# A hybrid attention and state space step: the pair mixing's Pool half on DVE, the norms' low parts on DVE, sums of squares by two additions

## The chip, the cores and the metric

One core of a Trainium2 chip runs the whole step. Its engines are TensorE (PE in the rows, PEld for its weight loads), VectorE (DVE), ScalarE (ACT), GpSimd (Pool) and SyncE (SP, which here issues the transfers). The metric is the device time of one execution in microseconds (us). Results are compared as medians of several runs.

## What is computed

One layer of a streaming encoder on 16 learned meta tokens, 2048 prompt frames and 64 new frames, 1024 wide, float32:

```python
q, k, v, u = project(h, p)            # pre-RMSNorm and one input projection
attn = swa_prompt(q, k, v, sinks)     # windowed attention, 8 query heads, 2 kv heads
y_ssm, fr, fi = s5_scan(u, h0_re, h0_im, p)   # 32 channel groups, each a 64-wide complex diagonal state
zs = gelu(y_ssm)
s_out = zs * sigmoid(zs @ w_glu + b_glu)
merged = concatenate([rmsnorm(attn, attn_out_g), rmsnorm(s_out, ssm_out_g)])
h = h + merged @ w_out
h = h + square(relu(rmsnorm(h, norm2_g) @ w_up)) @ w_down
```

The state space part is x[t] = a x[t-1] + B u[t] with complex a, then y = Re(C x) + D u. The kernel scans blocks of 8 tokens: 266 blocks (`NCH`), 258 of the prompt (`PCH`) and 8 of the new frames, which start from a given state.

## The kernel before

Products keep float32 accuracy by splitting each operand into a high part, rounded on ACT, and a low part, the difference between value and high part, and multiplying high by high, high by low and low by high. A low part is thus one two-input subtraction in SBUF on DVE or Pool.

The program runs through stages: the projection of u; attention, with the q, k, v projection, the tables of the state space part and the first products with `w_out`; the state space pairs; the gate (GLU) with the rest of the products with `w_out`; then the squared-ReLU MLP, more than half of the time.

The stage of the pairs works on sixteen pairs of channel groups. For pair j, SP loads U and `ra` (`ssm_load`: two matrices and two tables, a cosine and a sine for each block) and `rb` (`ssm_load2`). PE multiplies U into block inputs (`ssm_in`, L1244), ACT copies them from PSUM into `RI` (`ssm_align`, L1253). Then `ssm_mix(j, i)` runs in six steps. Step 0 multiplies `RI` by the cosine table (`o1`, L1263, DVE) and the sine table (`o2`, L1264, Pool), 2 x 266 columns each. Step 1 combines them into real and imaginary part (`ab`, L1266 on DVE, L1267 on Pool). Steps 2 and 3 scan each part along the blocks, 258 columns and then 8 (L1271, DVE). Step 4 multiplies the result by the two tables again (`p1`, L1275, DVE; `p2`, L1276, Pool). Step 5 writes H, the states at the block ends: two subtractions into partitions 0 to 63 (L1281, DVE), two additions into partitions 64 to 127 (L1284, Pool), and then two small copies on DVE (L1286, L1287). PE multiplies H and U into the output (`ssm_out`, L1293 and L1294), ACT copies it (L1299), SP stores it. `ssm_mixes` writes the steps of pair i among those of pair i - 1:

```python
for j, k in ((i, 0), (i - 1, 4), (i, 1), (i, 2), (i - 1, 5), (i, 3)):
```

Between the pairs PE fills its time with products of the attention half with `w_out`: `out` (L1452) sums an output tile in PSUM, `out_evac` adds it on DVE into `xo` (L1494), SP stores two of them together (L1455) and loads the next buffer (L1445). There are three `xo` buffers.

The norms ahead of `w_out` run on six blocks of 352 tokens, for the attention half ("a") and the gated half ("s"). `norm_square` squares on ACT (L1406) and sums four slices on DVE (L1408), PE sums over partitions (L1413), `norm_root` and `norm_newton` form the inverse root, and `norm_split` multiplies (L1434, DVE), rounds (L1435, ACT) and takes the low part (L1436, Pool), each twice per block, 704 columns. `wg_split` splits the gate's weights: high part on ACT (L1392), low part on Pool (L1393), two of 1024 columns.

The order of the instructions on each engine is not the order of writing: `Order.arrange` collects them all, gives each a cost by engine, size and kind, lets operations of DVE and Pool that share SBUF inputs exclude each other in time, and places them by a list schedule run backwards and forwards. A changed engine therefore means a new order for the whole program. SP, too, issues its transfers in that order, one behind the other.

Of the kernel before, what the change touches and what calls it, by code (L numbers as in the profile page):

```python
# [15 lines left out]
ALU = mybir.AluOpType  # L16
AX = mybir.AxisListType
# [31 lines left out]
def f32(ap):  # L49
    return ap.bitcast(F32)  # L50
# [326 lines left out]
def tile_trunk(ctx: ExitStack, tc: tile.TileContext, I, O, dbg=None, stop=None):  # L377
    nc = tc.nc
# [375 lines left out]
    xr, xh, xl, ss, rs = {}, {}, {}, {}, {}  # L754
# [500 lines left out]
    def ssm_mix(j, i):  # L1255

        x, sp, v, e = Sx[j], Sx["sp"], nc.vector, nc.gpsimd
        two = lambda a: a.unsqueeze(1).broadcast_to((P, 2, NCH))
        tc_, ts_ = two(x["ra"][:, 2 * P : 2 * P + NCH]), two(x["ra"][:, 2 * P + NCH :])
        wide = lambda n: sp.tile([P, 2, NCH], F32, tag=n, name=n)  # L1260
        if i == 0:
            x["o1"], x["o2"], x["ab"] = (wide(n) for n in ("o1", "o2", "ab"))
            v.tensor_mul(x["o1"], x["RI"], tc_)  # L1263
            e.tensor_mul(x["o2"], x["RI"], ts_)  # L1264
        elif i == 1:
            v.tensor_add(x["ab"][:, 0], x["o1"][:, 0], x["o2"][:, 1])  # L1266
            e.tensor_sub(x["ab"][:, 1], x["o1"][:, 1], x["o2"][:, 0])  # L1267
        elif i in (2, 3):
            c = i - 2
            for lo, hi, init in ((0, PCH, 0.0), (PCH, NCH, g0[:, c, j : j + 1])):  # L1270
                v.tensor_tensor_scan(out=x["ab"][:, c, lo:hi], data0=r8[:, j : j + 1].broadcast_to((P, hi - lo)),  # L1271
                                     data1=x["ab"][:, c, lo:hi], initial=init, op0=ALU.mult, op1=ALU.add)
        elif i == 4:
            x["p1"], x["p2"] = wide("p1"), wide("p2")
            v.tensor_mul(x["p1"], x["ab"], tc_)  # L1275
            e.tensor_mul(x["p2"], x["ab"], ts_)  # L1276
        elif i == 5:
            H = x["H"] = GH[j % 2]
            for gg in range(2):
                r = slice(64 * gg, 64 * gg + 64)  # L1280
                v.tensor_sub(H[0:64, gg, 1:], x["p1"][r, 0], x["p2"][r, 1])  # L1281
            for gg in range(2):
                r = slice(64 * gg, 64 * gg + 64)
                e.tensor_add(H[64:, gg, 1:], x["p1"][r, 1], x["p2"][r, 0])  # L1284
            gs = slice(2 * j, 2 * j + 2)
            v.tensor_copy(Sx["fin"][:, :, gs].rearrange("p q g -> p g q"), H[:, :, PCH : NCH + 1 : NCH - PCH])  # L1286
            v.tensor_copy(H[:, :, PCH], Sx["h0"][:, gs])  # L1287
# [27 lines left out]
    def ssm_mixes(i):  # L1315

        for j, k in ((i, 0), (i - 1, 4), (i, 1), (i, 2), (i - 1, 5), (i, 3)):
            if pair_ok(j):
                ssm_mix(j, k)
# [69 lines left out]
    def wg_split(k):  # L1389
        h, l = (w[:, 2 * k : 2 * k + 2] for w in WO["g"])  # L1390
        raw = WO.pop(("g", k))
        nc.scalar.copy(h, raw)  # L1392
        nc.gpsimd.tensor_sub(l, raw, f32(h))  # L1393

    def norm_x(t, n):
        x = WO["na"].tile([P, 4, OB], F32, tag="x", name="x")
# [6 lines left out]
    def norm_square(t, n):  # L1403
        x = N[t, n]
        sq = WO["na"].tile([P, 4, OB], F32, tag="x", name="sq")
        nc.scalar.activation(sq, x["x"], AF.Square)  # L1406
        x["ss"] = WO["na"].tile([P, OB], F32, tag="t", name="ss", bufs=1)
        nc.vector.tensor_reduce(out=x["ss"], in_=sq.rearrange("p k n -> p n k"), axis=AX.X, op=ALU.add)  # L1408

    def norm_sum(t, n):  # L1410
        x = N[t, n]
# [16 lines left out]
    def norm_split(t, n):  # L1428
        x = N[t, n]
        a, y = x.pop("x"), x.pop("y")  # L1430
        h, l = (WO["na"].tile([P, 4, OB], F32R, tag="x" + i, name="x" + i) for i in "hl")
        x["h"], x["l"] = h, l
        for ks in (slice(0, 2), slice(2, 4)):
            nc.vector.tensor_mul(a[:, ks], a[:, ks], y.unsqueeze(1).broadcast_to((P, 2, OB)))  # L1434
            nc.scalar.copy(h[:, ks], a[:, ks])  # L1435
            nc.gpsimd.tensor_sub(l[:, ks], a[:, ks], f32(h[:, ks]))  # L1436

    hv = hd.rearrange("e p n -> p e n")
    
# [86 lines left out]
    for t, f in ((26, a2_open), (27, lambda: norm_square("a", 0)), (28, lambda: norm_sum("a", 0)), (28, lambda: norm_root("a", 0)), (28, lambda: norm_newton("a", 0)),  # L1526
                 (28, wo_open), (29, lambda: norm_split("a", 0)), (28, lambda: wo_split(0, 0)), (28, lambda: wo_split(0, 1)),
                 (29, lambda: wo_split(0, 2)), (29, lambda: wo_split(0, 3)), (29, lambda: norm_load(1)), (30, lambda: wg_row(0)), (30, lambda: wg_row(1)), (31, lambda: norm_square("a", 1)),
                 (31, lambda: wg_split(0)), (32, lambda: wg_split(1)), (32, lambda: norm_sum("a", 1)), (32, lambda: norm_root("a", 1)), (33, lambda: norm_newton("a", 1)), (33, lambda: norm_split("a", 1))):
        jobs.setdefault(t, []).append(f)  # L1530
# [8 lines left out]
    for s in range(NC_ + 2):  # L1539
# [47 lines left out]
        for f in jobs.get(s, ()):  # L1587
# [15 lines left out]
    Sx["pr"] = lambda: prs.tile([P, OB], F32, tag="r", name="psr")  # L1603
    norm_load(2)
    do = {"load": norm_load, "square": lambda n: norm_square("a", n), "sum": lambda n: norm_sum("a", n),
          "root": lambda n: norm_root("a", n), "newton": lambda n: norm_newton("a", n), "split": lambda n: norm_split("a", n)}
    after = {}
    for i, fs in ((-2, "square 2"), (-1, "sum 2, root 2"), (0, "newton 2, split 2, load 3"), (2, "square 3"), (3, "sum 3, root 3"),
# [227 lines left out]
    v, e = nc.vector, nc.gpsimd  # L1836
# [421 lines left out]
```

## Time and profile before

| what | us |
|---|---|
| median of 3 runs | 2190.11 (2185.74 to 2190.66) |
| profiled execution | 2188.35, its span 2186.6 |
| PE busy | 2030.3 (93%) |
| DVE busy | 1888.7 (86%) |
| ACT busy | 1259.2 (58%) |
| Pool busy | 592.9 (27%) |
| stage of the pairs, 485 to 656 | 171, of it DVE busy 151.6, PE 133.8, Pool 107.6 |

Busy time is the time in which at least one instruction of the engine runs; an engine can be busy and yet wait inside an instruction. A row of groups gives line, engine, operation, output and inputs, shape and count, then busy time and mean length of one (ns), then the idle time of the engine ahead of the group and what ended it. A row of a source line gives shortest, median and longest execution in ns. A row of a timeline gives start and length in us.

### The profile page before, as it was taken

To read this page: it belongs to the slowest core of one execution; us is meant where nothing else is said; L and a number is where in the kernel's file an instruction comes from. 1 tells how busy PE (TensorE), PEld (TensorE's weight loads), DVE (VectorE), ACT (ScalarE), POOL (GpSimd) and SP (SyncE) were. 2 spreads that over 40 slices of the span, in tenths; PEclk is the share of its full clock that TensorE was granted. 3 is DMA by queue.
4 is the path that set the end of the run, shared out by engine and by line. 5 is a ranking of instruction groups with operands and counts; after the bars stand their busy time and mean duration, and the time that the engine had idled before them with its cause. 6 is when DMAs were issued, how large, how long until landed. Compare 5 with 4: busy or idle time off the path is not lost.

```text
span 2186.6 us, 35316 instructions
## 1 busy us (share of the span) xinstructions
PE 2030.3 (93%) x12230; PEld 1950.7 (89%) x12230; DVE 1888.7 (86%) x3378; ACT 1259.2 (58%) x2560; POOL 592.9 (27%) x670
## 2 busy tenths in 40 slices
PE   8989989898866997999999999999999999999999
PEld 7978888787655996999989989999999999999999
DVE  8969999988985787899999998888977988888778
ACT  6447777863325463665555566665555765555554
POOL 7943211035660434554334441200000200000000
PEclk9999999989988997999999999999999999999999
DMA  6532223447662466654564667645744774444432
GB/s 220 136 67 80 69 74 86 151 156 225 225 196 69 126 194 216 201 190 151 175 219 164 225 210 248 202 144 161 254 152 140 223 226 138 136 140 137 142 122 92
DMA packets 306164, 354.46 MB, mean 162 GB/s; under 512 B 28737, under 2 KB 216768, under 8 KB 305474
## 3 DMA queue, kind: packets, MB, share of 16 engines
q1 hardware_dynamic: 305842, 352.21, 51.4%
q8 instruction: 97, 1.59, 0.3%
q14 instruction: 81, 0.66, 0.1%
q10 hardware_dynamic: 144, 0.00, 0.0%
HBM read 260.15 MB, written 94.07 MB: 162 GB/s over the span
## 4 chain that ended last, share of the span: by engine, by line
PE 58%; DVE 26%; DMA 5%; issue 5%; ACT 4%; SPq 1%; POOL 0%; DVEq 0%; ACTq 0%; POOLq 0%
PE psd L2066 24%; PE bB L1971 9%; PE bA L1971 8%; PE bC L1971 7%; PE pso L1452 3%; DVE acc L2075 2%; DVE ul L1961 2%; PE psqkv L906 2%; DVE hl L2054 2%; PE psg L1670 1%; PE pu L811 1%; DMA hd<-xo 1%; DVE M L1142 1%; PE pv L1184 1%; DVE wl L2035 1%
## 5 line engine op out<-in xcount | busy, mean ns | idle before, releaser
L2066 PE MATMUL psd<-hh,wh 128*128 128x352 f32 x1344 | 434.6, 324 | 11.6 <-DVE acc L2075 10.0
L2066 PE MATMUL psd<-hl,wh 128*128 128x352 f32 x1344 | 431.7, 322 | 2.1 <-DVE hl L2054 1.9
L2066 PE MATMUL psd<-hh,wl 128*128 128x352 f32 x1344 | 429.9, 321 | 0.2 <-DVE wl L2035 0.2
L2075 DVE TENSOR_TENSOR acc<-psd,acc 128x352 f32<-128x352 f32 x624 | 315.2, 517 | 36.5 <-PE psd L2066 36.1
L2066 PEld LDWEIGHTS psd<-hh,wh 128*128 128x128 f32 x1344 | 252.0, 188 | 17.6 <-DVE acc L2075 12.0
L2066 PEld LDWEIGHTS psd<-hl,wh 128*128 128x128 f32 x1344 | 252.6, 188 | 2.9 <-DVE hl L2054 2.9
L2066 PEld LDWEIGHTS psd<-hh,wl 128*128 128x128 f32 x1344 | 252.2, 188 | 0.4 <-DVE wl L2035 0.4
L2034 ACT CAST wh<-d 128x512 fp32r<-128x512 f32 x240 | 146.7, 617 | 43.1 <-PE psd L2066 35.2
L1960 ACT CAST uh<-ur 128x512 fp32r<-128x512 f32 x144 | 89.1, 620 | 141.5 <-PE bC L1971 66.8
L1971 PE MATMUL bA<-xh,uh 128*128 128x352 f32 x480 | 158.6, 330 | 8.7 <-DVE hid L1989 5.1
L1971 PE MATMUL bA<-xl,uh 128*128 128x352 f32 x480 | 155.8, 325 | 3.6 <-DVE xl L1789 3.6
L1960 ACT CAST uh<-us 128x512 fp32r<-128x512 f32 x128 | 79.4, 621 | 134.8 <-PE bB L1971 68.6
L1971 PE MATMUL bB<-xh,uh 128*128 128x352 f32 x480 | 155.8, 325 | 1.0 <-DVE hid L1989 1.0
L1971 PE MATMUL bB<-xh,ul 128*128 128x352 f32 x480 | 155.3, 324 | 0.9 <-DVE ul L1961 0.9
L1971 PE MATMUL bA<-xh,ul 128*128 128x352 f32 x480 | 156.1, 325 | 0.0
L906 PE MATMUL psqkv<-wqa,xh 128*128 128x384 f32 (+1 forms) x544 | 150.3, 354 | 5.8 <-ACT z L919 5.5
L1971 PE MATMUL bB<-xl,uh 128*128 128x352 f32 x480 | 154.5, 322 | 0.0
L2035 DVE TENSOR_TENSOR wl<-d,wh 128x512 fp32r<-128x512 f32 x208 | 144.4, 694 | 1.2 <-ACT wh L2034 1.1
L1990 ACT ACTIVATE hid<-hid 128x352 f32<-128x352 f32 x144 | 71.6, 499 | 121.1 <-DVE hid L1989 115.6
L2054 DVE TENSOR_TENSOR hl<-hid,hh 128x352 fp32r<-128x352 f32 x240 | 139.6, 582 | 0.0
L1971 PE MATMUL bC<-xl,uh 128*128 128x352 f32 x384 | 125.1, 326 | 7.0 <-DVE xl L1789 7.0
L1961 DVE TENSOR_TENSOR ul<-ur,uh 128x512 fp32r<-128x512 f32 x144 | 109.1, 758 | 24.3 <-ACT uh L1960 24.3
(450 smaller groups left out, 5803.2 us busy)
## 6 DMA issues: line engine op xcount, KB each, us to landing
ur<-in_w_up_dram SPq DMA_DIRECT2D x160, 256.0 KB
d<-in_w_down_dram SPq DMA_DIRECT2D x128, 256.0 KB
us<-usd SPq DMA_DIRECT2D x128, 256.0 KB
d<-dsd SPq DMA_DIRECT2D x96, 256.0 KB
hd<-xo SPq DMA_DIRECT2D x48, 352.0 KB
usd<-s SPq DMA_DIRECT2D x64, 256.0 KB
dsd<-d SPq DMA_DIRECT2D x48, 256.0 KB
dx<-in_w_down_dram SPq DMA_DIRECT2D x48, 256.0 KB
```

The lines of the kernel that those rows point to most:

```text
L811: nc.tensor.matmul(ps[m], w[:, c], x[:, k % 2], start=(k == 0 and i == 0), stop=(k == KT - 1 and i == 2))
L906: nc.tensor.matmul(t["ps"][c][:n, :384], x, w[k][:, c * 384 : c * 384 + 384], start=(k == 0 and i == 0), stop=(k == KT - 1 and i == 2))
L1452: nc.tensor.matmul(ps, w, x, start=(i == 0), stop=(i == len(seq) - 1))
L1960: nc.scalar.copy(h, src)
L1961: nc.vector.tensor_sub(l, src, f32(h))
L1971: nc.tensor.matmul(ps, w[:, k], x[:, k], start=(p in BANK and k == 0 and a == 0), stop=False, skip_group_check=True)
L1990: nc.scalar.activation(h, h, AF.Relu)
L2034: nc.scalar.copy(h, src)
L2035: (e if p in POOLED[i >= NPR] else v).tensor_sub(l, src, f32(h))
L2054: eng.tensor_sub(l, src, f32(h))
L2066: nc.tensor.matmul(ps, w[:, c], y, start=(p in DFIRST and n == 0), stop=False, skip_group_check=True)
L2075: v.tensor_add(ACC[eh, nh][:, x], ps, ACC[eh, nh][:, x])
```

## The change

Eight instructions move or change. In `ssm_mix` the five Pool instructions of a pair are issued on DVE. In `wg_split` and `norm_split` the low part is taken on DVE. In `norm_square` the reduction over four slices becomes an addition of two slices to two, in place, and an addition of the two results. Nothing else is edited; the order is planned anew.

```diff
             v.tensor_mul(x["o1"], x["RI"], tc_)
-            e.tensor_mul(x["o2"], x["RI"], ts_)
+            v.tensor_mul(x["o2"], x["RI"], ts_)
...
-            e.tensor_sub(x["ab"][:, 1], x["o1"][:, 1], x["o2"][:, 0])
+            v.tensor_sub(x["ab"][:, 1], x["o1"][:, 1], x["o2"][:, 0])
...
-            e.tensor_mul(x["p2"], x["ab"], ts_)
+            v.tensor_mul(x["p2"], x["ab"], ts_)
...
-                e.tensor_add(H[64:, gg, 1:], x["p1"][r, 1], x["p2"][r, 0])
+                v.tensor_add(H[64:, gg, 1:], x["p1"][r, 1], x["p2"][r, 0])
...
-        nc.gpsimd.tensor_sub(l, raw, f32(h))
+        nc.vector.tensor_sub(l, raw, f32(h))
...
-        nc.vector.tensor_reduce(out=x["ss"], in_=sq.rearrange("p k n -> p n k"), axis=AX.X, op=ALU.add)
+        nc.vector.tensor_add(sq[:, 0:2], sq[:, 0:2], sq[:, 2:4])
+        nc.vector.tensor_add(x["ss"], sq[:, 0], sq[:, 1])
...
-            nc.gpsimd.tensor_sub(l[:, ks], a[:, ks], f32(h[:, ks]))
+            nc.vector.tensor_sub(l[:, ks], a[:, ks], f32(h[:, ks]))
```

## Rows read from the trace of the kernel before

**Rows 1.** Table of stretches, stage of the pairs: length, busy time and count per engine, granted clock, DMA.

```profile
485.00:656.00 171.00, 133.77 (x633) 112.82 (x632) 151.57 (x238) 51.64 (x96) 107.58 (x88) 0.92 0.70 220
```

**Rows 2.** Groups of DVE instructions, 484 to 660 us: mixing and the norms' multiply.

```profile
L1271 DVE TENSOR_TENSOR_SCAN ab<-r,ab 128x258 f32<-128x258 f32 x32 | 25.1, 784 | 0.1
L1275 DVE TENSOR_TENSOR p<-ab,ra 128x532 f32<-128x532 f32 x16 | 23.7, 1483 | 0.0
L1281 DVE TENSOR_TENSOR H<-p,p 64x266 f32<-64x266 f32 x32 | 18.9, 590 | 0.3
...
L1271 DVE TENSOR_TENSOR_SCAN ab<-r,g,ab 128x8 f32<-128x8 f32 x32 | 17.7, 554 | 0.0
L1263 DVE TENSOR_TENSOR o<-RI,ra 128x532 f32<-128x532 f32 x16 | 11.2, 698 | 0.2 <-ACT RI L1253 0.2
L1266 DVE TENSOR_TENSOR ab<-o,o 128x266 f32<-128x266 f32 x16 | 10.4, 648 | 0.0
L1434 DVE TENSOR_TENSOR x<-x,y 128x704 f32<-128x704 f32 x8 | 10.4, 1314 | 0.0
...
L1286 DVE COPY fin<-H 128x4 f32<-128x4 f32 x16 | 7.0, 437 | 0.6 <-POOL H L1284 0.6
L1287 DVE COPY H<-h 128x2 f32<-128x2 f32 x16 | 6.9, 434 | 0.3
```

**Rows 3.** Groups of Pool instructions, 484 to 660 us: the norms' low part.

```profile
L1436 POOL TENSOR_TENSOR xl<-x,xh 128x704 fp32r<-128x704 f32 x8 | 15.7, 1971 | 3.3 <-ACT xh L1435 3.3
```

**Rows 4.** Source lines over the whole span: shortest, median, longest execution in ns.

```profile
L1271 DVE TENSOR_TENSOR_SCAN ab<-r,ab x32: 677/682/2066, 490.7 to 651.1; 128x258 f32<-128x258 f32 x32
L1271 DVE TENSOR_TENSOR_SCAN ab<-r,g,ab x32: 203/552/1145, 492.7 to 651.7; 128x8 f32<-128x8 f32 x32
...
L1275 DVE TENSOR_TENSOR p<-ab,ra x16: 703/1724/1760, 499.6 to 651.9; 128x532 f32<-128x532 f32 x16
...
L1281 DVE TENSOR_TENSOR H<-p,p x32: 420/432/893, 503.1 to 654.2; 64x266 f32<-64x266 f32 x32
...
L1286 DVE COPY fin<-H x16: 156/158/1642, 510.4 to 655.5; 128x4 f32<-128x4 f32 x16
...
L1287 DVE COPY H<-h x16: 152/463/1181, 510.9 to 655.7; 128x2 f32<-128x2 f32 x16
...
L1434 DVE TENSOR_TENSOR x<-x,y x24: 878/893/2384, 440.3 to 808.1; 128x704 f32<-128x704 f32 x24
```

**Rows 5.** Timelines of DVE and then Pool, last pairs: start, length, what.

```profile
635.75 0.43 DVE L1281 TENSOR_TENSOR H<-p,p 64x266 f32<-64x266 f32 x1
636.19 1.62 DVE L1271 TENSOR_TENSOR_SCAN ab<-r,ab 128x258 f32<-128x258 f32 x1
...
637.86 0.69 DVE L1263 TENSOR_TENSOR o<-RI,ra 128x532 f32<-128x532 f32 x1
638.48 1.72 DVE L1275 TENSOR_TENSOR p<-ab,ra 128x532 f32<-128x532 f32 x1
...
645.91 1.72 DVE L1275 TENSOR_TENSOR p<-ab,ra 128x532 f32<-128x532 f32 x1
...
638.02 1.61 POOL L1276 TENSOR_TENSOR p<-ab,ra 128x532 f32<-128x532 f32 x1 [0.76 <-DVE ab L1271]
```

**Rows 6.** Waits, 484 to 660 and (SP queue) 470 to 670 us: total, times, longest.

```profile
DVE xo L1494 <- PE pso L1452: 15.0, 9, 3.9
...
SPq L1445 <- DMA hd<-xo: 28.8, 9, 7.4
```

**Rows 7.** Timelines of DVE and PE in the attention stage.

```profile
421.38 2.67 DVE L1408 TENSOR_REDUCE ss<-sq 128x352 f32<-128x1408 f32 x1 [0.72 <-ACT sq L1406]
...
425.84 0.47 PE L1138 MATMUL pm<-KB,QT 128*128 128x256 f32 x2 [2.80 <-DVE M L1142]
```

**Rows 8.** Timelines of Pool and DVE in the attention stage.

```profile
444.77 3.85 POOL L1436 TENSOR_TENSOR xl<-x,xh 128x704 fp32r<-128x704 f32 x2 [53.62 <-ACT xh L1435]
...
446.36 0.69 DVE L1174 TENSOR_TENSOR el<-e,eh 128x512 fp32r<-128x512 f32 x1
```

## The prediction, made before the result was known

> **What bounds the kernel now.** I read the table of stretches first, to find where the touched work lies. Nearly all of it is in the stage of the sixteen state space pairs, 485 to 656 us. There DVE is busy 151.6 of 171 us, PE 133.8, Pool 107.6, ACT 51.6 and the DMA engines 0.70 of the time [rows 1]: DVE is the bound, with 19.4 us of idle time. What ended most of that idle time is the second thing to see: in the table of waits the DVE accumulation of an output tile waits 15.0 us for PE, and the SP queue holds nine loads of output tiles for 28.8 us until an earlier store of the same buffer has landed [rows 6]. So the stage is a DVE queue that is full nine tenths of the time and now and then starved by transfers.
>
> Third, the groups of DVE instructions in that stage [rows 2] beside the shortest execution of the same lines [rows 4]. They differ widely: the multiply by the cosine table takes 1.48 us on average and 0.70 at best, the eight-step scan 0.55 and 0.20, the copy of the final state 0.44 and 0.16. The timeline says why [rows 5]: the 1.72 us multiply at 638.48 lies beside Pool's own multiply of 1.61 us that began at 638.02, while the multiply of the same size at 637.86, after Pool's previous operation had ended, took 0.69. DVE is busy, but much of its busy time is waiting for Pool.
>
> **What the change does, in the pair's mixing.** Per pair, five instructions leave Pool for DVE: the two multiplies by the sine table, one subtraction of 266 columns, two additions into H. Both engines' halves then cost one undisturbed DVE price each. From the shortest executions [rows 4]: four multiplies at 0.70, two 266-column combinations at 0.42 (the price of H's, which has as many columns), two long scans at 0.68, two short at 0.20, four H writes at 0.42, two copies at 0.16: 2.81 + 0.84 + 1.35 + 0.41 + 1.68 + 0.31 = 7.40 us. Before, the eight mixing groups sum to 11.2 + 10.4 + 25.1 + 23.7 + 18.9 + 17.7 + 7.0 + 6.9 = 120.9 us [rows 2], 7.56 a pair. Consecutive instructions overlap: the one at 637.86 ends at 638.55, the next began at 638.48 [rows 5], 0.07 us. I take 0.06 for each instruction, fifteen after and eleven before: 7.40 - 0.90 = 6.50 against 7.56 - 0.66 = 6.90, so 16 x 0.40 = 6.4 us less. That is one end. The other is that the four H writes, one after another, don't overlap: the H write at 635.75 of 0.43 us is followed only at 636.19 [rows 5]. Four H writes and the instruction behind them without overlap give back five times 0.06, 0.3 a pair, 4.8 us in all, and leave 1.6. I take 5.0, nearer to the first end, because the kernel's order places the steps of two pairs between each other, so that dependent steps rarely stand side by side. The last pairs, where little else runs, give a second look: one pair every 7.43 us (638.48 to 645.91 [rows 5]) against 6.5.
>
> The Trainium skill ("VectorE: DVE Perf Modes", section "Two Vector instructions with no wait between them") says that an instruction whose input or output begins in another group of 32 partitions than the last one's starts only when all earlier ones have finished. H's four writes read partitions 0 and 64 and write 0 and 64, so by that rule the dear end of the sum is the right one; the row of 635.75 agrees for the one write it shows. It stands as the third rival below.
>
> **Who waits.** Pool is left without work in this stage, so its waits go (each of its steps stood behind a DVE step and was followed by one). On the new path nothing waits for another engine between the aligned copy by ACT and H; what is late next is the load of U and of the tables, and DVE itself. Queued behind the added steps on DVE are the accumulations of PE's output tiles; PE waits for those if they come late. The last pair gains about 1 us, the difference of the two periods above.
>
> **Norms.** In this stage 8 of the 24 low-part subtractions come from Pool (2.0 us each [rows 3]) to DVE: 704 columns, the size of the norm's multiply, 0.88 at best [rows 4], 0.82 with overlap: +6.6. The multiplies themselves lose their stretch, 1.31 to 0.88: 8 x 0.43 = -3.5. Each sum of squares was one reduction of 2.67 us [rows 7]; it becomes an addition of 704 columns (0.88) and one of 352, 0.52 (an estimate from 0.42 for 266 columns and 0.88 for 704), less overlap 1.3: -1.35, three times here: -4.0. Together -0.9. No DMA and no wait on a queue moves with any of this; SP's and Pool's queues carry nothing of it.
>
> Outside the stage: two of the reductions stand near the end of the attention stage. The one at 421.38 holds DVE for 2.67 us, and PE's next score product began 2.80 us late behind a DVE maximum queued after it [rows 7]; two reductions at 1.35 less give 2.6 if all of it shows, none if it is hidden; I take 2.0. Against it, four low parts (3.3 us) and the two splits of the gate weights (1024 columns; 1.2 each scaled from 0.88, 2.4 in all) enter DVE's queue between 444 and 477. They are needed only by later products, so most of it lies in DVE gaps; I charge 0.5 of 5.7, the whole being the bound. In the GLU stage six reductions shrink (-8) and twelve low parts come (+10), with PE the busy engine there; I count nothing, bounds -2 to +3. The squared-ReLU MLP behind has none of the edits.
>
> Sum: 5.0 + 1.0 + 0.9 + 2.0 - 0.5 = 8.4 us. The profiled execution took 2188.35 us (span 2186.6 and 1.75 around it), 1.8 below the median of the three runs, 2190.11. **Forecast: 2188.35 - 8.4 = 2180 us**, 0.46% below the median. The bounds of its terms (mixing 1.6 to 6.4, reductions 0 to 2.6, low parts up to 5.7, GLU -2 to +3) give 2174 to 2191.
>
> **The rule on the shared port.** Rows first: of DVE's nine groups in the stage, the seven lines with a shortest execution shown hold 45 us above it (12.5 the cosine multiply, 11.2 short scans, 5.4 H, 4.5 and 4.5 the copies, 3.5 the norm multiply, 3.4 long scans: counts times mean less shortest [rows 2, 4]). That is what Pool's 107.6 us cost DVE. But a DVE subtraction of 512 columns took 0.69 us at 446.36, inside a Pool pair of operations that ran from 444.77 for 3.85 us [rows 8]: Pool does not stretch everything. The Trainium skill ("SBUF — State Buffer", section "SBUF: two separate sides") says that DVE operations with two inputs in SBUF and GpSimd hold one port pair exclusively, and the loser waits for the whole operation. By that rule all 45 us go and the sum above stands; the row at 446.36 does not agree with it, that at 638.48 does.
>
> **Rivals.** (1) *DVE alone becomes the longer queue.* Added to DVE in the stage: per pair two multiplies, one combination and two H writes, less overlap, 0.64 + 0.36 + 0.64 + 0.72 = 2.36, 37.8 us for sixteen, plus 6.6 low parts, less 4.0 for the reductions: 40.4 us. The change loses in the stage as soon as less than 40.4 of the 45 us were Pool's doing. For it: 446.36, and that the second scan and the copies, where most of the stretch sits, might wait for DVE's own earlier results. Against it: 637.86 beside 638.48. If 26 of the 45 go, DVE is 14 us longer, accumulations come later, and the time is 2188 + 14 - 2 = **2200**, slower. Chance 0.18.
>
> (2) *Transfers set the stage.* DVE's saved time turns into idle time because the SP queue still holds the loads behind landing stores for 28.8 us [rows 6], and a pair's tables come no sooner. Then 171 us stay and only the outside terms count: 2188.35 - 1.5 = **2187**. For it: DMA engines 0.70 busy and all of DVE's longer gaps end with PE. Against it: DVE has no gap for nine tenths of the stage. Chance 0.18.
>
> (3) *H's writes never overlap.* Each of the four and the instruction behind them starts only when the one before has ended, as behind the row of 635.75 [rows 5]: mixing saves 1.6 instead of 5.0, 3.4 less, **2183.5**. Chance 0.10. The Trainium skill's rule on held instructions, cited above, asks for this one.
>
> (4) *The gaps shrink too.* With Pool out of a pair's path H is ready sooner, PE is held less, and the planned order, which no longer has to guess Pool's times, fits better. If half of the 19.4 us of idle time goes: **2170**. Chance 0.10.
>
> (5) *The order is rewritten and eats it.* All instructions are placed by a list scheduler whose costs for these steps change, so the order elsewhere may change and the kernel comes out where it was, 2186 to 2192. The rows show nothing either way. Chance 0.06.
>
> **How the numbers follow.** Forecast 0.38, rivals 0.18, 0.18, 0.10, 0.10, 0.06. A measurement of this kernel can tell about 0.3%, 6.6 us, from no change: faster lies below 2183.5, slower above 2196.7. Faster: of the forecast's own 0.38 some 0.34, rival 4 whole, a little of rival 3: 0.47. Slower: rival 1 and a little of 5: 0.19. The rest, 0.34, is the same. The range: 2167 takes in rival 4, 2199 most of the way to rival 1; about one in ten lies beyond each end. The forecast's own range is 2174 to 2191.
>
> **What would show it.** Right: between 485 and about 650 Pool has no instruction; the cosine multiply and its sine twin both take 0.70 with no long ones; the short scan is 0.20, the copies 0.16; DVE's busy time in the stage falls to about 146 us though it has some 90 more instructions; the stage is about 165 us; a pair in the tail takes 6.5 us. Sums of squares: 0.88 and 0.52 where 2.67 stood. Wrong if short scans and copies keep their means (rival 1), if DVE's gaps behind PE and SP's holds grow by what DVE saved (rival 2), if the four H writes stand end to end at 0.43 (rival 3), or if the MLP's stretch alone grows.

## The result: 2140.5 us where 2190.3 stood

The changed kernel takes 2140.54 us (median of 4 runs, 2137.64 to 2142.49), the kernel before 2190.32 in the same comparison: ratio 0.9776, 95% interval 0.9759 to 0.9794, some 49 us less. The prediction was 2180, range 2167 to 2199: the sign was right, the size was not, and the time lies below the range.

The stretches say where it went. I cut both traces at the same four points: the first product of a pair (`ssm_in`), the last output of a pair (`ssm_out`), the first gate product, the first product of the MLP. First the kernel before, at these cuts (columns: busy time and count of PE, PEld, DVE, ACT, Pool, then granted clock, DMA share and GB/s):

```profile
482.50:659.30 176.80, 138.84 (x653) 116.57 (x653) 153.13 (x240) 54.34 (x102) 107.58 (x88) 0.92 0.69 219
659.30:671.40 12.10, 0.36 (x3) 0.01 (x1) 1.31 (x2) 3.67 (x5) 0.00 (x0) 0.68 0.70 241
671.40:832.10 160.70, 152.01 (x881) 146.69 (x882) 122.31 (x159) 87.05 (x142) 57.82 (x37) 0.96 0.43 136
832.10:2182.10 1350.00, 1310.52 (x8072) 1296.33 (x8071) 1188.51 (x2125) 789.83 (x1596) 239.22 (x156) 0.99 0.55 175
```

Then the changed kernel, whose profiled span is 2139.4 us:

```profile
479.90:617.20 137.30, 107.07 (x480) 88.94 (x481) 133.54 (x311) 44.52 (x94) 0.00 (x0) 0.90 0.73 236
617.20:632.50 15.30, 15.10 (x94) 14.73 (x93) 8.45 (x15) 12.61 (x12) 0.00 (x0) 1.00 0.88 275
632.50:790.90 158.40, 155.62 (x946) 152.43 (x947) 118.77 (x185) 87.82 (x142) 34.27 (x26) 1.00 0.53 166
790.90:2135.20 1344.30, 1310.98 (x8072) 1297.87 (x8071) 1182.63 (x2127) 790.24 (x1596) 235.05 (x155) 0.99 0.56 176
```

The start, all that lies ahead of the stage of the pairs, moved by -2.6, the stage of the pairs by -39.5, the gap behind it by +3.2, the gate by -2.3, the MLP by -5.7: -46.9 of the 47.2 between the spans. In the stage, DVE's idle time fell from 23.7 to 3.8 us (length less busy) and its busy time by 19.6. The second line of each fence holds the other half of the story: PE did nothing in the gap before (0.36 of 12.1 us) and works all through it now (15.10 of 15.3).

DVE's groups in the stage of the changed kernel, against [rows 2]: count, busy time, mean ns, idle time ahead:

```profile
L1271 DVE TENSOR_TENSOR_SCAN ab<-r,ab 128x258 f32<-128x258 f32 x32 | 22.1, 691 | 0.4
L1284 DVE TENSOR_TENSOR H<-p,p 64x266 f32<-64x266 f32 x32 | 13.8, 431 | 0.4
L1281 DVE TENSOR_TENSOR H<-p,p 64x266 f32<-64x266 f32 x32 | 13.6, 426 | 0.6 <-PE psy L1294 0.4
L1495 DVE TENSOR_TENSOR xo<-pso,xo 128x352 f32<-128x352 f32 x24 | 12.1, 516 | 2.9 <-PE pso L1453 2.9
L1275 DVE TENSOR_TENSOR p<-ab,ra 128x532 f32<-128x532 f32 x16 | 11.3, 706 | 0.0
L1264 DVE TENSOR_TENSOR o<-RI,ra 128x532 f32<-128x532 f32 x16 | 11.3, 706 | 0.0
L1276 DVE TENSOR_TENSOR p<-ab,ra 128x532 f32<-128x532 f32 x16 | 11.3, 705 | 0.0
L1263 DVE TENSOR_TENSOR o<-RI,ra 128x532 f32<-128x532 f32 x16 | 11.2, 703 | 0.2 <-ACT RI L1253 0.2
L1271 DVE TENSOR_TENSOR_SCAN ab<-r,g,ab 128x8 f32<-128x8 f32 x32 | 7.0, 218 | 0.1
L1266 DVE TENSOR_TENSOR ab<-o,o 128x266 f32<-128x266 f32 x16 | 6.8, 428 | 0.0
L1267 DVE TENSOR_TENSOR ab<-o,o 128x266 f32<-128x266 f32 x16 | 6.8, 426 | 0.0
L1437 DVE TENSOR_TENSOR xl<-x,xh 128x704 fp32r<-128x704 f32 x6 | 5.3, 884 | 0.0
L1435 DVE TENSOR_TENSOR x<-x,y 128x704 f32<-128x704 f32 x6 | 5.1, 884 | 0.0
L1408 DVE TENSOR_TENSOR sq<-sq 128x704 f32<-128x704 f32 x3 | 2.7, 884 | 0.0
L1287 DVE COPY H<-h 128x2 f32<-128x2 f32 x16 | 2.5, 158 | 0.0
L1286 DVE COPY fin<-H 128x4 f32<-128x4 f32 x16 | 2.4, 153 | 0.0
...
L1409 DVE TENSOR_TENSOR ss<-sq 128x352 f32<-128x352 f32 x3 | 1.6, 521 | 0.0
```

Every price is the undisturbed one: the multiplies by the tables 0.71 where [rows 2] had 1.48 for one of them, the short scan 0.22 for 0.55, the copies 0.15 and 0.16 for 0.44. Yet the groups of the mixing still sum to 120.1 us (before 120.9): more instructions at lower prices. DVE's busy time fell for two other reasons: the 71 instructions more that it now has mostly overlap the one before by about 0.08 us each, and the rest of the list is shorter. Output tiles: 24 accumulations, 2.9 us of idle time ahead of them, where the same group before reads

```profile
L1494 DVE TENSOR_TENSOR xo<-pso,xo 128x352 f32<-128x352 f32 x38 | 18.8, 517 | 16.6 <-PE pso L1452 15.0 <-DMA xo<-in_xT_dram 1.5
```

So the attention half's products with `w_out`, all 38 of which stood among the pairs before, are now 24 there and 14 behind, in the gap in which PE was empty. Nothing in the diff says so; the list schedule did it.

What the idle time looked like before is seen in the timeline of the kernel before, DVE, Pool and PE, from 519 us (start, length, what; in brackets idle time and its releaser):

```profile
519.10 0.70 DVE L1263 TENSOR_TENSOR o<-RI,ra 128x532 f32<-128x532 f32 x1
519.27 1.61 POOL L1276 TENSOR_TENSOR p<-ab,ra 128x532 f32<-128x532 f32 x1 [3.05 <-DVE ab L1271]
520.22 2.09 PE L1244 MATMUL pss<-U,ra 128*128 128x266 f32 x4 [2.03 <-DMA ra<-reca]
523.23 0.53 DVE L1494 TENSOR_TENSOR xo<-pso,xo 128x352 f32<-128x352 f32 x1 [3.42 <-PE pso L1452]
525.42 0.53 DVE L1494 TENSOR_TENSOR xo<-pso,xo 128x352 f32<-128x352 f32 x1 [1.67 <-PE pso L1452]
525.86 0.70 DVE L1275 TENSOR_TENSOR p<-ab,ra 128x532 f32<-128x532 f32 x1
```

PE waits for a table, the output tile behind that wait is late, and DVE stands 3.42 and 1.67 us in front of the accumulations of that tile and the next. The pair's multiply at 525.86 is queued behind them although its input was there: Pool's multiply of the same `ab` ran at 519.27.

### The profile page after: what moved, and what is told of

Its sections match the earlier page's. It is cut to its first block, busy times and chain, and to the rows that moved or that the text cites. A ratio compares the mean times of both kernels' runs of the same rounds, so it can differ in the third digit from the quotient of the medians.

```text
span 2139.4 us, 35227 instructions
## 1 busy us (share of the span) xinstructions
PE 2021.8 (95%) x12230; PEld 1949.0 (91%) x12230; DVE 1864.9 (87%) x3496; ACT 1258.8 (59%) x2560; POOL 445.1 (21%) x564
## 4 chain that ended last, share of the span: by engine, by line
PE 66%; DVE 23%; DMA 4%; ACT 3%; issue 3%; SPq 0%; POOL 0%; DVEq 0%; ACTq 0%; POOLq 0%
PE psd L2067 26%; PE bB L1972 9%; PE bA L1972 9%; PE bC L1972 8%; PE pso L1453 3%; PE psqkv L906 3%; DVE ul L1962 2%; PE psg L1671 2%; PE pv L1184 2%; DVE acc L2076 1%; DVE hl L2055 1%; DVE ss L785 1%; DVE ab L1271 1%; PE s L1162 1%; DVE uT L817 1%
## 5 line engine op out<-in xcount | busy, mean ns | idle before, releaser
L2067 PE MATMUL psd<-hh,wh 128*128 128x352 f32 x1344 | 434.3, 324 | 13.3 <-DVE acc L2076 10.4
```

Of the source, the lines that this page charges most:

```text
L2067: nc.tensor.matmul(ps, w[:, c], y, start=(p in DFIRST and n == 0), stop=False, skip_group_check=True)
```

## The experiments

Theory before them: the stage's pace was set by the planned order, which spaced the pairs out to keep operations of DVE and Pool apart, and the new order carries the gain. Rival: the engines' prices do, in a way that I had undersized. Ratios are to the kernel before, run beside each.

**All moves without the new sums.** The change less its edit of `norm_square`.

```diff
-        nc.vector.tensor_add(sq[:, 0:2], sq[:, 0:2], sq[:, 2:4])
-        nc.vector.tensor_add(x["ss"], sq[:, 0], sq[:, 1])
+        nc.vector.tensor_reduce(out=x["ss"], in_=sq.rearrange("p k n -> p n k"), axis=AX.X, op=ALU.add)
```

> All moves from Pool to DVE, with the sum of squares still one reduction. Both theories below: the reduction is worth little, 2140 to 2146 us (twelve times 1.35 us less on DVE, of which few stand on the path). If the two additions carried a large part of the gain, 2150 or more.

2148.58 us, 0.9805 (0.9789 to 0.9822), between the two ranges. The moves make most of it; the sums are worth some 8 us on top (6 by the two ratios; these kernels were not run side by side).

**Engines alone.** The moves, but each moved instruction goes through the plan as if it were still Pool's; TensorE, ScalarE and SyncE keep the order of the kernel before, instruction for instruction.

```diff
-        eng = [str(i.engine).split(".")[-1] for i in L]
+        real = [str(i.engine).split(".")[-1] for i in L]
+        eng = ["Pool" if k in self.moved else e for k, e in enumerate(real)]
```

> The same moves with the reduction as before, but the planner costs and places the moved instructions as if they were still on Pool, so PE, ACT and SP run exactly the order of the kernel before and DVE runs the moved instructions at the places in time that Pool had. Theory 'order' (most of the 49 us comes from the new order, in which output tiles leave the stage of the pairs and DVE no longer stands behind accumulations that wait for PE): 2172 to 2186, DVE idle in the stage 25 us or more. Theory 'port' (most comes from Pool no longer holding DVE up): 2145 to 2160, the stage near 145 us even with all its output tiles.

2188.54 us, 0.9994 (0.9984 to 1.0003): no change, and even less than theory 'order' allowed. DVE's idle time in the stage is 17.5 us, not 25 or more.

**Order alone.** The reverse: the work stays on Pool, the plan takes it for DVE's; the three other engines have the order of the moves' kernel, instruction for instruction.

```diff
+        eng = ["DVE" if k in self.moved else e for k, e in enumerate(real)]
```

> The moved instructions stay on Pool, but are costed and placed as if they were on DVE, so PE, ACT and SP run exactly the order of the moved version (with the old reduction). Theory 'order': clearly faster than before, 2150 to 2175, since the order alone brings most. Theory 'port': 2190 to 2215, because Pool and DVE disturb each other as before in an order that doesn't reckon with it.

2158.11 us, 0.9853 (0.9838 to 0.9868). With the work on Pool as before, 32 of the moves' 42 us are there, as theory 'order' said. The four kernels, all with the old sums (us):

| | order planned for Pool | order planned for DVE |
|---|---|---|
| the moved work on Pool | 2190.5 (before) | 2158.1 |
| the moved work on DVE | 2188.5 | 2148.6 |

The stage of the pairs in the three new kernels, in the order told (same columns as above):

```profile
478.20:620.50 142.30, 110.44 (x497) 90.62 (x498) 138.38 (x311) 46.35 (x97) 0.00 (x0) 0.90 0.73 231
```

```profile
488.80:657.70 168.90, 136.64 (x653) 115.59 (x653) 151.43 (x328) 53.96 (x101) 0.00 (x0) 0.94 0.71 229
```

```profile
481.40:629.80 148.40, 112.52 (x500) 92.80 (x499) 142.91 (x226) 46.38 (x97) 96.00 (x86) 0.89 0.70 222
```

From Pool to DVE takes 7.9 us off the stage in the old order (176.8 to 168.9) and 6.1 in the new (148.4 to 142.3); the order takes off 28.4 with Pool at work and 26.6 without. In the third kernel DVE is idle for 5.5 us, though the rows of the same stretch show it stretched by Pool as ever:

```profile
L1283 DVE TENSOR_TENSOR p<-ab,ra 128x532 f32<-128x532 f32 x16 | 21.4, 1339 | 0.0
L1289 DVE TENSOR_TENSOR H<-p,p 64x266 f32<-64x266 f32 x32 | 21.1, 661 | 0.3
```

So Pool was not what spaced the pairs out; the plan was. These lengths are of single executions, and they hang on when the stage began. Counted from the start of the program to the end of the stage, moving the engines is worth 1.6 us in the old order and 9.3 in the new, as the whole times have it (1.9 and 9.5): Pool's price shows once the pace is gone. (Engines alone shortened the stage by 7.9 us and the whole by 2: in that execution the stage began 6.3 us later, and up to there DVE was busy for 428.5 us instead of 422.9, the low parts of the attention stage. How much of the 6.3 they cost is open, since the kernel with tiles held back, below, whose order up to there is that of the kernel before, began the stage 3.8 later as well.)

**Mixing alone**, the norms' low parts left on Pool.

```diff
-        nc.vector.tensor_sub(l, raw, f32(h))
+        nc.gpsimd.tensor_sub(l, raw, f32(h))
...
-            nc.vector.tensor_sub(l[:, ks], a[:, ks], f32(h[:, ks]))
+            nc.gpsimd.tensor_sub(l[:, ks], a[:, ks], f32(h[:, ks]))
```

(and the old sum of squares)

> Only the pairs' mixing moves to DVE; low parts on Pool and reduction as before. Both theories: most of the gain, 2140 to 2155. If the low parts or the reduction made the difference in the MLP (7 us) too, the MLP here takes as long as before; if the new order around the stage did it, it is short here as well.

2167.12 us, 0.9896 (0.9874 to 0.9917), about half of the gain, where both theories had most of it; its stage is 140.2 us, about as short as that of all moves, its MLP 1351.4, as long as before.

**Low parts alone**, and **the sums alone**: the other two parts of the change, each by itself in the kernel before.

> The kernel before with one part of the change: the low parts of the norms and of the gate weights on DVE, planned so; the pair's mixing stays on Pool and the sums of squares stay reductions. Theory (the order carries the gain; each part's order gain adds up): mixing alone gave 2167 and mixing with low parts 2149, so low parts should be worth some 12 to 18 us by themselves, most of it in the MLP's stretch (about 7 us shorter) and at the end of attention: 2172 to 2180, with the stage of the pairs still 170 to 177 us long. Rival (low parts are dear on DVE by their price and gain only where the mixing has left Pool): 24 x 0.82 us more on DVE and the old pace of the pairs, 2188 to 2196.

2172.64 us, 0.9925 (0.9909 to 0.9941). The stage of the pairs is 166.7 us, below what was expected, the MLP 1341.2, 8.8 shorter than before, though no line of that stretch is edited. In the kernel with the order alone, which keeps the low parts on Pool, the MLP is as short:

```profile
811.00:2152.60 1341.60, 1304.65 (x8073) 1291.55 (x8072) 1181.12 (x2126) 790.43 (x1597) 239.47 (x156) 0.99 0.56 176
```

So the MLP's share, too, comes with the order.

> The kernel before with the sums of squares by two additions, and nothing else of the change. Theory of prices: twelve reductions of 2.67 us become 0.88 and 0.52, 1.3 us less each with overlap; the moves with and without it differed by 8 us, 5 of them in the stage of the pairs and 5 in the gate's, so alone it should give about the same there, 2180 to 2184. Rival (DVE's time is worth little as long as the old pace of the pairs leaves it 24 us idle in the stage): 2 us in attention and up to 5 in the gate's stage, the stage of the pairs within 3 us of 176.8: 2184 to 2190.

2187.96 us, 0.9994 (0.998 to 1.0008): the rival's time. The shorter sums give nothing alone and 8 us on top of the moves, where the stage went from 142.3 to 137.3 and the gate from 163.9 to 158.4. Its stages were not as the rival said: the stage of the pairs is 170.9 us, 5.9 shorter, and begins 8.5 later, in an execution of 2193.21 us, 5 above the kernel's median. In the gate's stage the saving does show as idle time: DVE is busy for 113.4 us there instead of 122.3, and the stage, 159.4, is 1.3 shorter.

**Is it the place of the output tiles?** Two kernels: the changed one with all 38 tiles of the attention half forced among the pairs, and the one before with its last 14 held back in the plan until the pairs are over.

```diff
+        for j, k in self.after:
+            m = -(-len(self.outs) * (j + 1) // 16)
+            deps[k] += self.outs[:m]
```

> The changed kernel, but its planner must place all 38 remaining output tiles of the attention half inside the stage of the pairs, spread evenly, as the order of before did (the changed kernel has 24 there and 14 behind). Theory 'fills' (the stage is long because those products and accumulations are in it, and PE then has nothing to do while the gate waits for its first input): the stage 160 us or more, the whole 2160 to 2180. Theory 'pace' (the old order is slow because the planner spread it to make DVE and Pool exclude each other): the stage 142 to 150 us, some PE idle time behind it, the whole 2146 to 2156.

2152.94 us, 0.9828 (0.9802 to 0.9854): 12 us lost, 37 kept, as theory 'pace' has it (its stage 1.8 longer).

```diff
-        out_mm(n, e, hf, ps)
+        with order.hold(590 if hf == (0,) and len(queue) - 8 * NOB < 14 else 0):
+            out_mm(n, e, hf, ps)
```

> The kernel before, Pool's work as it was, but the last 14 output tiles of the attention half are held back in the plan until the pairs are through. Theory 'fills': the stage falls to 150 us or less, the whole to 2155 to 2170. Theory 'pace': the stage stays at 165 to 177 us although 14 tiles are gone from it; the whole 2178 to 2195.

2192.84 us, 1.0015 (1.0002 to 1.0027): nothing gained, as theory 'pace' has it. The stretches of both, the pairs and the gap behind them, the forced one first:

```profile
477.80:629.60 151.80, 125.49 (x636) 112.03 (x637) 144.39 (x331) 53.89 (x102) 0.00 (x0) 0.94 0.77 243
629.60:645.50 15.90, 0.45 (x3) 0.03 (x1) 1.34 (x2) 3.70 (x5) 0.00 (x0) 0.64 0.85 285
```

```profile
486.30:655.00 168.70, 124.00 (x498) 96.82 (x499) 151.74 (x227) 54.11 (x102) 108.79 (x88) 0.82 0.63 201
655.00:668.70 13.70, 13.70 (x86) 13.47 (x84) 3.73 (x6) 3.63 (x4) 0.00 (x0) 1.00 0.75 248
```

With tiles held back, PE is full in the gap, and yet the stage is still 168.7 us: PE did less in it, and DVE still stood idle for 17.0. In the changed kernel with all tiles forced in, DVE is idle for 7.4 of 151.8 us. In the new pace the place of the tiles is worth about a quarter (12 of 49 us), in the old one nothing. The pace itself can be read off one instruction: `p1` (L1275) comes every 10.2 us on average before, at distances between 6.0 and 17.1, and every 8.3 us in the changed kernel. A rival is that any new plan moves the time by luck. But the plan with tiles held back and that of the sums alone were made anew too, and moved it by less than 4 us.

**Is it the plan's exclusion?** The kernel before, every instruction on its engine, but in the plan the moved ones no longer exclude DVE. (In the plan every operation of Pool excludes nearly every operation of DVE that works in SBUF alone.)

```diff
-            port[k] = self.ported(i, e, ws, rs, dma[k])
+            port[k] = self.ported(i, e, ws, rs, dma[k]) and k not in self.moved
```

> The kernel before, every instruction on its engine, Pool included; only in the plan the moved Pool instructions no longer exclude DVE's (cost and engine as before). Theory 'pace': the exclusion in the plan is what spread the pairs; without it the stage is 145 to 155 us and the whole 2150 to 2170 although Pool and DVE still hold each other up. If the exclusion in the plan does no harm: 2185 to 2200, since the order then ignores a contention that the chip has.

2176.47 us, 0.9936 (0.9913 to 0.9959), between the two ranges; the stage is as theory 'pace' said:

```profile
483.40:635.50 152.10, 111.21 (x491) 95.15 (x491) 148.99 (x227) 48.33 (x97) 101.15 (x87) 0.87 0.69 218
```

In the stage, dropping the exclusion takes off 24.7 us, nearly all of the 28.4 that planning the work as DVE's takes off with Pool at work: most of the old spacing is the exclusion. Of the whole it makes 14 us; planning the work as DVE's, at DVE's shorter cost and in one queue, makes 32. Behind the stage the gate, with the tiles that left the pairs, takes 169.0 us (167.2 with the order alone), and the MLP is 3.6 us shorter than before (8.4 with the order alone). What that rest owes to the longer cost that the plan gives Pool's instructions, and what to the one queue, was not tried.

And the changed kernel without any exclusion in its plan (the line above taken out):

> The changed kernel, every instruction on its engine as there; only the plan is different: what is left on Pool (the MLP's start and its low parts) and DVE no longer exclude each other in it anywhere. Theory (an order that doesn't space the work out for Pool is the better one, wherever Pool's work is): the MLP's start is packed closer, 2125 to 2140. Rival (the exclusion is true of the chip for what is left, so that an order without it runs into the stretch it ignores): 2140 to 2155.

2171.04 us, 0.9915 (0.99 to 0.993): 30 us lost, more than the rival said. The stage of the pairs, now without Pool, is unchanged at 136.9 us; it begins 13.8 us later, the gate takes 165.2 for 158.4, the MLP 1352.1 for 1344.3. Where Pool still works, an order that knows nothing of it is worse. That theory, as I had widened it, fell.

**More of Pool's work to DVE.** First the steps at the start of the MLP: its slow gain multiplies, two subtractions, a low part and the sums of squares.

```diff
-            nc.gpsimd.tensor_mul(x, x, M["rs"][:, nh].unsqueeze(1).broadcast_to((P, 2, OB)))
+            nc.vector.tensor_mul(x, x, M["rs"][:, nh].unsqueeze(1).broadcast_to((P, 2, OB)))
...
-            nc.gpsimd.tensor_add(HS[n], sq[:, 0], sq[:, 1])
+            nc.vector.tensor_add(HS[n], sq[:, 0], sq[:, 1])
```

> The changed kernel with Pool's steps at the start of the MLP moved to DVE as well (the slow gain's multiplies, two subtractions, one low part, and the sums of squares of h). If the lesson of the first runs holds there too (a faster chain and an order without exclusion): 5 to 10 us faster than the changed kernel, 2131 to 2136. If DVE, which is 97 to 99% busy right behind, becomes the bound: equal or slower, 2140 to 2148.

2144.11 us, 0.9792 (0.9768 to 0.9816): no gain over the change, as its second case has it. Then also the low parts inside the MLP:

```diff
-    POOLED = (2, 6, 4), ()
+    POOLED = (), ()
...
-                        x_cut(ORD[q], r, XS[2 * q + r], v if r else e)
+                        x_cut(ORD[q], r, XS[2 * q + r], v)
```

> The changed kernel with nearly all that Pool still does in the MLP moved to DVE too: its slow gain multiplies, low parts and sums of squares, and the pooled part of the later products' operands. Theory (Pool's exclusion in the plan is what costs; with Pool nearly empty there is none left): 2130 to 2142. Rival (in the MLP, DVE is 88 per cent busy and PE 97 per cent, so each microsecond given to DVE there delays its evacuations): 2145 to 2165.

2112.23 us, 0.965 (0.9636 to 0.9665): faster than both kernels, 28 us below the change, and below both ranges. The MLP of the changed kernel had PE idle for 33.3 us (above); here it is 14.8:

```profile
782.60:2105.80 1323.20, 1308.40 (x8132) 1302.27 (x8132) 1172.34 (x2204) 791.70 (x1597) 136.35 (x88) 1.00 0.57 181
```

DVE took over 48 low parts of the weights, 14 of the operands and the steps of the last run, and is busy for 10 us *less* than in the changed kernel. To part engine and order here as well, two kernels between the last two (plan and engines crossed, as in the second and third run):

> The two last edits that led from the kernel with more work on DVE (2144) to the one with Pool nearly empty (2112) are 32 low parts of the MLP's second weights and the low parts of its next operands, from Pool to DVE. Here they run on DVE, but stand where the plan would have put them on Pool: the orders of TensorE, ScalarE and SyncE are those of the 2144 us kernel. Theory A (as in the stage of the pairs, the new order carries the gain and the engines alone next to nothing): 2136 to 2146. Theory B (in the MLP it is the engines' price, Pool's 2 us instructions stretching those of DVE beside them): 2112 to 2122.

Engines alone: 2134.06 us, 0.9744 (0.9726 to 0.9763), 10 us below the 2144 of the kernel that they start from. (The expectation counts 32 low parts; the rows of Pool show 48.)

> The counterpart: the two edits' work stays on Pool, but the plan takes it for DVE's, so that TensorE, ScalarE and SyncE have the order of the 2112 us kernel. Theory A (the order carries the gain): 2110 to 2122. Theory B (the engines' price): 2136 to 2150.

Order alone: 2131.63 us, 0.9733 (0.9716 to 0.9749), 12.5 us below it. Neither theory's numbers: both together make 32, so each gives about a third and the last third needs both. The group that shows the engines' share is the low parts of the hidden values, on DVE throughout, untouched by the edits. In the new order, with the 62 low parts on Pool, and then with them on DVE:

```profile
L2069 DVE TENSOR_TENSOR hl<-hid,hh 128x352 fp32r<-128x352 f32 x240 | 147.7, 620 | 1.0 <-ACT hh L2068 1.0
```

```profile
L2055 DVE TENSOR_TENSOR hl<-hid,hh 128x352 fp32r<-128x352 f32 x240 | 128.9, 537 | 0.4 <-ACT hh L2054 0.4
```

83 ns of 620 for each of 240 instructions go with them. In the old order the same step takes off 34 of 576.

## Why the prediction was wrong, point by point

**What bounds the kernel: half right.** DVE's idle time behind PE and behind SP's holds [rows 1, 6] was seen, and named "now and then starved by transfers". At these cuts it was 23.7 of 176.8 us, and 19.9 of it went: half of what the stage lost. SP's holds were not what set the stage (rival 2): SP still stands before the loads of output tiles for 24.4 us in the changed kernel, against 28.8, and the stage is 39.5 us shorter.

**Mixing, -5.0: right.** Engines alone took DVE's busy time in the stage from 153.13 to 151.43, with 7.1 us of low parts added, 3.5 taken off the norm's multiplies (10.4 to 6.9), and 1.0 more in the accumulations: 6.3 for the mixing, inside 1.6 to 6.4. For all moves together that is 1.7 us of DVE's busy time in the old order; in the new one (third kernel to first) it is 142.91 - 138.38 = 4.5. The sum behind rival 1 set some 45 us of Pool's doing against 44.4 added (40.4 without the 4.0 that the sums spare). Its first figure was right: with the work on DVE in the old order the seven lines lost some 44 us. The two nearly balance. Two slips in the sums change little: a pair has sixteen instructions on DVE after the change, not fifteen, so that the cheap end is 7.4, not 6.4; and the bounds of the terms add up to 2175 and 2194, not 2174 and 2191.

**H's writes: rival 3's mechanism is true, its price was not.** A timeline of the changed kernel, DVE:

```profile
560.38 0.43 DVE L1267 TENSOR_TENSOR ab<-o,o 128x266 f32<-128x266 f32 x1
560.73 0.87 DVE L1281 TENSOR_TENSOR H<-p,p 64x266 f32<-64x266 f32 x2
561.61 0.88 DVE L1284 TENSOR_TENSOR H<-p,p 64x266 f32<-64x266 f32 x2
562.52 0.70 DVE L1271 TENSOR_TENSOR_SCAN ab<-r,ab 128x258 f32<-128x258 f32 x1
...
564.12 0.70 DVE L1263 TENSOR_TENSOR o<-RI,ra 128x532 f32<-128x532 f32 x1
564.74 0.71 DVE L1264 TENSOR_TENSOR o<-RI,ra 128x532 f32<-128x532 f32 x1
565.36 0.71 DVE L1275 TENSOR_TENSOR p<-ab,ra 128x532 f32<-128x532 f32 x1
```

Four writes in 1.79 us, end to end, at 0.42 to 0.44 each; the first still overlaps the instruction before it by 0.08, so four starts a pair are held and not five. The Trainium skill's rule on instructions that are held ("VectorE: DVE Perf Modes", "Two Vector instructions with no wait between them") agrees with these rows. The other instructions overlap by 0.08 (564.12 to 564.74 at 0.70), not by 0.06, which pays for it: 120.1 / 16 = 7.51 less twelve times 0.08 is 6.5 a pair, for 6.50 predicted. The look at the tail has its counterpart in the kernel with the engines alone, whose order is the old one: there the multiplies that stood 7.43 apart stand 6.85 apart (640.15 and 647.00), for 6.5 predicted.

**Norms, -0.9: right in price.** Sums of squares 0.88 and 0.52, low parts and multiplies 0.88, as sized. What was not sized is that 1.3 us less per sum is worth next to nothing in the old order (1.5 us, within the noise) and some 8 us in the new.

**Outside the stage.** Attention's -2.0 and +0.5 can't be told from the scatter of its end (-2.6 in the changed kernel). The gate's 0 (-2 to +3) was -2.3, just beyond its bound. The MLP "has none of the edits" and still gave 5.7: the run with the order alone, 8.4 us shorter there, shows that the order did it.

**The step that failed** is the one ahead of all terms: the sum kept the old order, its 38 tiles among the pairs and its 19.4 us of gaps, and priced the edits inside it. For that kernel the total was nearly right: without its sums of squares (4.0 and 2.0) it says 2186, and engines alone took 2188.54. Part of that is luck: the stage gave 7.9 us where the terms say 2.9, and the later start took 6.3 back. But that kernel is not what was built. In its place the runs show the new order: by itself, with all work left on Pool, it is worth 32 us (2158.11), a term that the sum put at nothing. Rival 5 named the rewritten order, gave it 0.06, looked only at a loss, and said that the rows show nothing either way. They did: DVE idle for 15.0 us in front of accumulations [rows 6] while, at 525.86 in the timeline above, a ready step of a pair stood behind them, and, in a stretch that I didn't open, a PE with 0.36 us of work in 12.1 us right behind a stage stuffed with 38 of its tiles. Rival 4 had the right place and half the size: the gaps shrank by 19.9, not 9.7, and 14 tiles left with them.

**The shared port.** With the work on Pool in the new order the cosine multiply takes 1.34 on average, on DVE alone 0.71: Pool stretches DVE, as the row at 638.48 [rows 5] had it. The Trainium skill's rule ("SBUF — State Buffer", "SBUF: two separate sides") fits that row. The prediction held the row at 446.36 [rows 8] against the rule; that was misread, for Pool's pair is two instructions, and the second began beside that DVE subtraction:

```profile
444.77 1.68 POOL L1436 TENSOR_TENSOR xl<-x,xh 128x704 fp32r<-128x704 f32 x1 [53.62 <-ACT xh L1435]
446.41 2.21 POOL L1436 TENSOR_TENSOR xl<-x,xh 128x704 fp32r<-128x704 f32 x1
```

Here it is Pool that was held: 2.21 us for the second, 1.68 for the first of the same size, 0.53 more beside a subtraction of 0.69. What the stretch is worth is another matter: moving the work off Pool frees 4.5 us of DVE in a stage of 148, since the moved work needs some 40 us of DVE itself.

Left open: what the 18 us of the order's 32 that dropping the exclusion does not give owe to the plan's cost for Pool and to the one queue, and why engines and order need each other for the last 10 of the MLP's 32 us.

## What to carry to other kernels

When a planner places the instructions, an edit has two effects, the price on the engines and the new plan, and the second can be the larger by far (here 32 us against 2 in the old order; in the new one the engines, too, were worth 10): look for what a new order could fill (an engine empty beside a stage crowded with its work, a queue standing in front of something while ready work waits behind it) and give that a term of its own. Cross engines and order in two kernels to part them; here that took two runs and settled which of them carried the gain. A saving on an engine that is paced by something else can show as idle time, and come back once the pace is gone, as the shorter sums did.

## What the runs showed of the hardware

Taking 62 low parts off Pool in the MLP made DVE's busy time there fall, though DVE does them all itself. With TensorE, ScalarE and SyncE in the same order it is 1190.90 us with them on Pool, for 2142 instructions,

```profile
784.20:2124.00 1339.80, 1312.83 (x8133) 1301.33 (x8132) 1190.90 (x2142) 791.93 (x1597) 233.13 (x150) 1.00 0.57 179
```

and 1172.34 with them on DVE, for 2204 (the row of the 2112 us kernel above). That Pool's work could cost DVE more than the work itself costs there, with DVE busy for 88% of the time, I had not expected. TensorE's granted clock followed the gap: 0.64 and 0.68, a mixture of its two levels (1.2 and 2.4 GHz), in the 12 to 16 us in which PE was empty behind the pairs, and 1.00, the upper level, where tiles filled it.
